# Softmax minus one-hot over 8192 rows: moving the middle blocks' loads and stores from two queues to one

## The chip, the cores and the metric

The kernel runs on one core of one Trainium2 chip. The metric is device time in microseconds (us); lower is better. The core has four compute engines that matter here: VectorE (DVE in the profile), ScalarE (ACT), GpSimd (POOL) and, for a tiny transpose at the start, TensorE (PE). SyncE (SP) only issues transfers. Data moves between the off-chip memory (HBM) and the on-chip memory (SBUF, 128 partitions) over 16 DMA engines. Two engines issue transfers in this kernel, SP and ACT, each into a queue of its own: the profile calls SP's queue q1 and ACT's q10. A transfer is issued by an instruction in its engine's stream, so an engine that waits before an issue holds up whatever stands behind it in that stream.

## What is computed

This is the backward pass of a cross-entropy loss. For each of 8 x 1024 rows of 8192 logits, the output is the row's softmax, less 1 at the place of the row's label.

```python
def reference(logits, labels):
    logits_max = np.max(logits, axis=-1, keepdims=True)
    exp_logits = np.exp(logits - logits_max)
    softmax = exp_logits / np.sum(exp_logits, axis=-1, keepdims=True)
    ...
    one_hot[batch_idx, seq_idx, labels] = 1.0
    return (softmax - one_hot).astype(np.float32)
```

Logits and output are float32, 268.4 MB each; every element is read once and written once.

## The kernel before, in words

The 8192 rows of the matrix are cut into 32 blocks of 256 rows (`B = 32`). Within a block, partition p holds the rows 2p and 2p+1, which lie one after the other in HBM. The kernel calls `t = 2b` and `u = 2b + 1` the two "rows" of block b: a row is thus a tile of 128 partitions x 8192 elements, 4 MB, one run of 32 KB for each partition. A whole block is 8 MB, one run of 64 KB for each partition.

The tile `X` (line 47) has three slots of one block each (`SLOTS = 3`). Block b uses slot b mod 3, and all the work is done in place: the logits are loaded into `X`, overwritten by exponentials, scaled, the one-hot subtracted, and the result is stored from the same place. So block b+3 can be loaded only once block b has been stored.

`by_block(b)` (line 258) writes out the work of a block in one fixed order:

- GpSimd and VectorE build the one-hot rows, GpSimd for the last 2048 columns (`hot_pool`), VectorE for the first 6144 (`hot`, in PSUM), as bytes packed four to a word.
- VectorE takes the row's maximum (`m`), which is where the row's load is waited for; ScalarE takes the exponential and its sum (`s`); VectorE takes the reciprocal (`r`).
- VectorE scales and subtracts in 6144 columns (`finish_dve`). The other 2048 are scaled by GpSimd for row t and by ScalarE for row u, and GpSimd subtracts (`subtract_pool`).
- `move(b)` issues the block's stores and a later block's loads. In the last block row t's store is issued as soon as it is finished, ahead of `move`.

All waits are written by hand through `run` (line 72), which puts an instruction on an engine with the semaphores that it waits for. `finished[t]` holds what a store of row t waits for (VectorE's and GpSimd's last results), `stored[t]` what a load into the same place waits for, `loaded[t]` what the maximum waits for. `got` and `put` are the semaphores of loads and stores.

Six row loads are issued on SP at the start (three blocks). Then, by `move` (line 154):

- Blocks 0 and 1: the two rows are stored on ACT, one transfer each. After block 0, block 3's two rows are loaded on SP, each when the row three blocks before it has been stored.
- Blocks 2 to 25 (`TURN <= b < RETURN`): the block is stored in two halves at once, the even partitions on SP and the odd ones on ACT (`halves`, line 124), each 64 runs of 64 KB. Behind each store, on the same queue, the half load of block b+2 is issued, which waits until its own half of block b-1 has been stored. After block 25, block 28's rows are also loaded on SP.
- Blocks 26 to 31: rows are stored on ACT, and on SP row t+6 is loaded when row t has been stored.

Which places of `move` set the order matters below:

```python
            if TURN <= b < RETURN:
                store(ts, halves)
                load([t + G * (SLOTS - 1) for t in ts], halves)
            else:
                for t in ts:
                    if t not in stored:
                        store([t], [(nc.scalar, every)])
            if b < TURN - 1 or b >= RETURN - 1:
                for t in ts:
                    if t + G * SLOTS < T:
                        load([t + G * SLOTS], [(nc.sync, every)])
```

Of the kernel before, what the change touches and what calls it, by code (L numbers as in the profile page):

```python
# [7 lines left out]
P = 128  # L8
G = 2
SLOTS = 3  # L10


TURN, RETURN = 2, 26
POOLED = 2048
ONE = 56.0
BYTE = mybir.dt.float8e4
# [3 lines left out]
def kernel(  # L20
# [6 lines left out]
    nc = tc.nc  # L27
# [9 lines left out]
    T = N // P  # L37
# [27 lines left out]
    with tc.tile_critical():  # L65
        sem = tc.alloc_semaphore
        got = [[sem(f"got{i}{j}") for j in range(G)] for i in range(SLOTS)]
        put = [[[sem(f"put{i}{j}{h}") for h in range(2)] for j in range(G)] for i in range(SLOTS)]
        lab_got, dve, act, pe, pool = (sem(n) for n in ("lab_got", "dve", "act", "pe", "pool"))
        count = {}  # L70

        def run(engine, waits, counter, method, **operands):

            last = {}
            for counted, value in waits:
                last[counted.name] = counted, max(value, last.get(counted.name, (counted, 0))[1])
            waits = list(last.values())
            for w in waits[:-1]:
                engine.wait_ge(*w)  # L79
            instruction = getattr(engine, method)(**operands)  # L80
            for w in waits[-1:]:
                instruction._wait_ge(*w)
            step = 16 if method == "dma_start" else 1
            instruction.then_inc(counter, step)
            count[counter.name] = count.get(counter.name, 0) + step
            return counter, count[counter.name]
# [3 lines left out]
        w = run(nc.gpsimd, [], pool, "memset", ap=ident[:], constant=0.0)  # L90
# [12 lines left out]
        for j in range(G):  # L103
            w = run(
                nc.tensor, [w_ident, w_lab], pe, "transpose",
                out=lab_ps[:, j, :], in_=lab_f[:, j, :], identity=ident[:],
            )
        w_turned = run(nc.vector, [w], dve, "tensor_copy", out=lab_i[:], in_=lab_ps)

        def small(w, out, in0, scalar1, scalar2, op0, op1):  # L110
            return run(
                nc.vector, [w], dve, "tensor_scalar",
                out=out[:], in0=in0[:], scalar1=scalar1, scalar2=scalar2, op0=op0, op1=op1,
            )

        w = small(w_turned, low, lab_i, 1, None, Alu.bitwise_and, Alu.bypass)
        w = small(w, place, low, 255.0 * ONE, ONE, Alu.mult, Alu.add)
        w = small(w, low, lab_i, 2, None, Alu.bitwise_and, Alu.bypass)
        w = small(w, lab, low, 32767.5, 1.0, Alu.mult, Alu.add)
        w = run(nc.vector, [w], dve, "tensor_tensor", out=place[:], in0=place[:], in1=lab[:], op=Alu.mult)  # L120
        w = small(w, low, lab_i, 2, None, Alu.logical_shift_right, Alu.bypass)
        w_lab = run(nc.vector, [w], dve, "tensor_copy", out=lab[:], in_=low[:])

        halves = [(nc.sync, slice(0, P, 2)), (nc.scalar, slice(1, P, 2))]
        loaded, stored, finished = {}, {}, []
        stored[-1] = [(0, w_turned), (1, w_turned)]

        def load(ts, queues):
            b, js = ts[0] // G, slice(ts[0] % G, ts[-1] % G + 1)
            for queue, ps in queues:  # L130
                free = [w for t in ts for h, w in stored.get(t - G * SLOTS, []) if ps.step is None or h in (None, ps.start)]
                w = run(
                    queue, free, got[b % SLOTS][js.start], "dma_start",
                    out=X[ps, b % SLOTS, js, :], in_=x_b[b, ps, js, :],
                )
            for t in ts:
                loaded[t] = w

        def store(ts, queues):
            b, js = ts[0] // G, slice(ts[0] % G, ts[-1] % G + 1)  # L140
            for t in ts:
                stored[t] = []
            for h, (queue, ps) in enumerate(queues):
                w = run(
                    queue, [w for t in ts for w in finished[t]],
                    put[b % SLOTS][js.start][h], "dma_start",
                    out=o_b[b, ps, js, :], in_=X[ps, b % SLOTS, js, :],
                )
                for t in ts:
                    stored[t].append((ps.start, w))  # L150

        every = slice(None)

        def move(b):
            ts = [G * b, G * b + 1]
            if TURN <= b < RETURN:
                store(ts, halves)
                load([t + G * (SLOTS - 1) for t in ts], halves)
            else:
                for t in ts:  # L160
                    if t not in stored:
                        store([t], [(nc.scalar, every)])
            if b < TURN - 1 or b >= RETURN - 1:
                for t in ts:
                    if t + G * SLOTS < T:
                        load([t + G * SLOTS], [(nc.sync, every)])

        def row(t):
            return X[:, t // G % SLOTS, t % G, :]
# [12 lines left out]
        def row_max(t):  # L182
            maxima[t] = maximum([loaded[t]], m[:, t : t + 1], row(t))

        def row_max_around(t, between):
            w_first = maximum([loaded[t]], m_half[:, 0:1], row(t)[:, : V // 2])
            made = between()
            w_second = maximum([loaded[t]], m_half[:, 1:2], row(t)[:, V // 2 :])
            maxima[t] = run(
                nc.vector, [w_first, w_second], dve, "tensor_tensor",  # L190
                out=m[:, t : t + 1], in0=m_half[:, 0:1], in1=m_half[:, 1:2], op=Alu.min,
            )
            return made
# [12 lines left out]
        def one_hot_pool(t):  # L206
            last_pool[:] = [one_hot(nc.gpsimd, pool, last_pool, t, hot_pool[:, t % G, :], slice(PART, V // 4))]

        def scale_pool(t, w):
            x = row(t)[:, pooled]  # L210
            return run(
                nc.gpsimd, [w], pool, "tensor_scalar",
                out=x, in0=x, scalar1=r[:, t : t + 1], scalar2=None, op0=Alu.mult,
            )
# [11 lines left out]
        def one_hot_dve(t):  # L226
            return one_hot(nc.vector, dve, used.get(t % G, [w_words, w_lab]), t, hot[:, t % G, :], slice(0, PART))
# [10 lines left out]
        def row_exp(t):  # L238
            x = row(t)
            return run(  # L240
                nc.scalar, [maxima[t]], act, "activation",
                out=x, in_=x, func=Act.Exp, bias=m[:, t : t + 1], scale=1.0, accum_out=s[:, t : t + 1],
            )

        def row_recip(t, w):
            return run(nc.vector, [w], dve, "reciprocal", out=r[:, t : t + 1], in_=s[:, t : t + 1])

        def scale_act(t, w, c):
            x = row(t)[:, c]
            return run(  # L250
                nc.scalar, [w], act, "activation",
                out=x, in_=x, func=Act.Copy, bias=0.0, scale=r[:, t : t + 1],
            )
# [4 lines left out]
        def by_block(b):  # L258
            t, u = G * b, G * b + 1
            one_hot_pool(t)  # L260
            one_hot_pool(u)
            t_hot = one_hot_dve(t)
            u_hot = one_hot_dve(u)
            row_max(t)
            w_exp = row_exp(t)
            if b + 1 < B:
                row_max(u)
                t_sum = row_recip(t, w_exp)
                w_exp = row_exp(u)
                w_scaled = scale_pool(t, t_sum)  # L270
            else:
                t_sum = row_max_around(u, lambda: row_recip(t, w_exp))
                w_scaled = scale_act(t, t_sum, pooled)
                w_exp = row_exp(u)
            t_pool = subtract_pool(t, w_scaled)
            finished.append([finish_dve(t, [t_hot, t_sum]), t_pool])
            if b + 1 == B:
                store([t], [(nc.scalar, every)])
            u_sum = row_recip(u, w_exp)
            u_pool = subtract_pool(u, scale_act(u, u_sum, pooled))  # L280
            finished.append([finish_dve(u, [u_hot, u_sum]), u_pool])
            move(b)

        for t in range(G * SLOTS):
            load([t], [(nc.sync, every)])
        for b in range(B):
            by_block(b)
        for b in range(B - SLOTS, B):
            for t in (G * b, G * b + 1):
                for _, w in stored[t]:  # L290
                    nc.scalar.wait_ge(*w)


# [28 lines left out]
```

## Time and profile before

| | |
|---|---|
| time, median of 3 runs | 1258.59 us (1258.44 to 1258.67) |
| the profiled execution's own time | 1258.22 us |
| its span, first to last instruction | 1256.4 us |
| VectorE busy | 1101.3 us (88%) |
| GpSimd busy | 549.1 us (44%) |
| ScalarE busy | 529.1 us (42%) |
| row maximum on VectorE | 64 rows, 8.68 us each |
| scale and subtract on VectorE | 64 rows, 6.62 us each |
| exponential on ScalarE | 64 rows, 7.12 us each |
| DMA packets | 12343, of them 2064 under 512 B |

Some help with the views of the profile. The page divides the span into 40 slices of 31.4 us and gives the busy share of each in tenths, and the GB/s that the DMA engines moved. The windows do the same for stretches that one asks for; there each row has the stretch, its length, the busy time and (in brackets) the number of instructions of TensorE's matmuls and weight loads, VectorE, ScalarE and GpSimd, then the clock granted to TensorE, the DMA engines' busy share and GB/s. A packet is counted in the stretch in which it starts, so in stretches of a few microseconds share and rate can be off, and a share can be a little over 1. A line such as "DVE m L80 <- DMA X<-in_logits_dram: 109.4, 27, 8.9" reads: VectorE's instructions that write `m` waited for loads of `X` for 109.4 us in all, 27 times, 8.9 us at the longest. All compute instructions have line 80, where `run` issues them.

The transfers as issued (the last number is the median time from issue to landing):

```profile
X<-in_logits_dram SPq DMA_DIRECT2D x16, 4096.0 KB, 37.2
out_dram<-X ACTq DMA_DIRECT2D x16, 4096.0 KB, 35.5
out_dram<-X ACTq DMA_DIRECT2D x24, 27.0
out_dram<-X SPq DMA_DIRECT2D x24, 24.1
X<-in_logits_dram SPq DMA_DIRECT2D x24, 40.7
X<-in_logits_dram ACTq DMA_DIRECT2D x24, 46.1
```

The first two lines are rows, the other four the halves of blocks.

### The profile page before, as it was taken

To read this page: it belongs to the slowest core of one execution; us is meant where nothing else is said; L and a number is where in the kernel's file an instruction comes from. 1 tells how busy PE (TensorE), PEld (TensorE's weight loads), DVE (VectorE), ACT (ScalarE), POOL (GpSimd) and SP (SyncE) were. 2 spreads that over 40 slices of the span, in tenths; PEclk is the share of its full clock that TensorE was granted. 3 is DMA by queue.
4 is the path that set the end of the run, shared out by engine and by line. 5 is a ranking of instruction groups with operands and counts; after the bars stand their busy time and mean duration, and the time that the engine had idled before them with its cause. 6 is when DMAs were issued, how large, how long until landed. Compare 5 with 4: busy or idle time off the path is not lost.

```text
span 1256.4 us, 893 instructions
## 1 busy us (share of the span) xinstructions
PE 0.4 (0%) x2; PEld 0.3 (0%) x2; DVE 1101.3 (88%) x267; ACT 529.1 (42%) x162; POOL 549.1 (44%) x166
## 2 busy tenths in 40 slices
PE   0000000000000000000000000000000000000000
PEld 0000000000000000000000000000000000000000
DVE  7999878889888898888988889888898888999984
ACT  2444542345523455234553345533455333555432
POOL 2555522555335553355533455334553345544331
DMA  9999999999999999999999999999999999999998
GB/s 403 417 434 451 432 434 432 434 432 434 426 413 432 434 434 434 432 434 413 424 434 434 434 432 432 407 432 434 432 428 411 432 434 416 433 434 434 428 433 364
DMA packets 12343, 537.00 MB, mean 427 GB/s; under 512 B 2064, under 2 KB 2064, under 8 KB 2096
## 3 DMA queue, kind: packets, MB, share of 16 engines
q10 hardware_dynamic: 6192, 268.51, 50.1%
q1 hardware_dynamic: 6144, 268.44, 49.6%
q14 instruction: 7, 0.06, 0.0%
HBM read 268.50 MB, written 268.44 MB: 427 GB/s over the span
## 4 chain that ended last, share of the span: by engine, by line
DMA 54%; DVE 32%; ACT 9%; another core or an unknown queue 2%; POOL 1%; ACTq 0%; issue 0%; SPq 0%
DMA X<-in_logits_dram 48%; DVE m L80 21%; ACT X L80 9%; DVE X L80 8%; DMA out_dram<-X 6%; DVE hot L80 1%; POOL X L80 1%; DVE m_half L80 1%; ACTq L80 0%; DVE r L80 0%; SPq L80 0%; ACTq L79 0%; SPq L317 0%; SPq L65 0%
## 5 line engine op out<-in xcount | busy, mean ns | idle before, releaser
L80 ACT ACTIVATE X<-X,m 128x8192 f32<-128x8192 f32 x64 | 455.8, 7122 | 697.0 <-DVE m L80 697.0
L80 DVE TENSOR_REDUCE m<-X 128x1 f32<-128x8192 f32 x63 | 544.5, 8680 | 109.4 <-DMA X<-in_logits_dram 109.4
L80 POOL TENSOR_SCALAR X<-X,r 128x2048 f32<-128x2048 f32 x31 | 168.7, 5441 | 643.6 <-DVE r L80 643.6
L80 DVE SCALAR_TENSOR_TENSOR X<-X,r,hot 128x6144 f32<-128x6144 f32 x64 | 423.3, 6615 | 2.2
L80 POOL TENSOR_TENSOR X<-X,hot_pool 128x2048 f32<-128x2048 f32 x64 | 245.3, 3833 | 35.4 <-ACT X L80 28.4
L80 POOL TENSOR_SCALAR hot_pool<-words,lab,place 128x512 int32<-128x512 int16 x64 | 132.9, 2076 | 10.9 <-DVE lab L80 4.5
L80 DVE TENSOR_SCALAR hot<-words,lab,place 128x1536 int32<-128x1536 int16 x64 | 117.0, 1874 | 0.0
L80 ACT ACTIVATE X<-X,r 128x2048 f32<-128x2048 f32 x33 | 66.1, 2002 | 8.4 <-DVE r L80 8.4
L80 DVE RECIPROCAL r<-s 128x1 f32<-128x1 f32 x64 | 10.1, 159 | 18.2 <-ACT X L80 18.2
L80 DVE TENSOR_REDUCE m_half<-X 128x1 f32<-128x4096 f32 x2 | 8.8, 4410 | 3.8 <-DMA X<-in_logits_dram 3.8
L80 ACT ACTIVATION_READ_ACCUMULATOR X<-X,m 128x1 f32 x64 | 11.9, 186 | 0.0
L80 DVE CAST X<-lab_raw 32x256 f32<-32x256 int32 x1 | 0.4, 373 | 4.8 <-DMA lab_raw<-in_labels_dram 4.8
L80 ACT ACT_TABLE_LOAD x1 | 1.3, 1283 | 1.3 <-SPq L65 1.3
L80 POOL IOTA words<- 128x2048 int16 x1 | 1.8, 1823 | 0.0
L80 DVE TENSOR_TENSOR m<-m_half 128x1 f32<-128x1 f32 x1 | 1.6, 1598 | 0.0
L80 DVE TENSOR_SCALAR low<-lab_i 128x64 int32<-128x64 int32 x3 | 0.6, 195 | 0.1
L80 DVE CAST lab_i<-hot 128x64 int32<-128x64 f32 x1 | 0.2, 224 | 0.5 <-PE hot L80 0.5
L80 PE MATMUL hot<-ident,X 32*128 32x32 f32 x2 | 0.4, 299 | 5.2 <-DVE X L80 5.2
L80 POOL MEMSET ident<- 32x32 f32 x1 | 0.1, 115 | 0.5 <-SPq L65 0.5
L80 PEld LDWEIGHTS hot<-ident,X 32*128 32x128 f32 x2 | 0.3, 194 | 5.2 <-DVE X L80 5.2
L80 DVE TENSOR_TENSOR place<-place,lab 128x64 f32<-128x64 f32 x1 | 0.2, 224 | 0.0
L80 POOL TENSOR_SCALAR_AFFINE_SELECT ident<-ident 32x32 f32<-32x32 f32 x1 | 0.2, 202 | 0.1
(7 smaller groups left out, 1.0 us busy)
## 6 DMA issues: line engine op xcount, KB each, us to landing
X<-in_logits_dram SPq DMA_DIRECT2D x16, 4096.0 KB, 37.2
out_dram<-X ACTq DMA_DIRECT2D x16, 4096.0 KB, 35.5
out_dram<-X ACTq DMA_DIRECT2D x24, 27.0
out_dram<-X SPq DMA_DIRECT2D x24, 24.1
X<-in_logits_dram SPq DMA_DIRECT2D x24, 40.7
X<-in_logits_dram ACTq DMA_DIRECT2D x24, 46.1
lab_raw<-in_labels_dram ACTq DMA_DIRECT2D x1, 64.0 KB, 3.9
```

What stands on the lines that cost most here:

```text
L80: instruction = getattr(engine, method)(**operands)
```

## The change

The halves go. From block 3 on, every transfer is issued by SP, in one order. ACT issues only the row stores of blocks 0, 1 and 2.

- Blocks 0 to 2 (`TURN` is 3 now) are stored by row on ACT. After blocks 0 and 1, blocks 3 and 4 are loaded by row on SP.
- Blocks 3 to 25: one transfer stores the whole block, the next loads the whole of block b+2, both on SP, 128 runs of 64 KB each. The load waits for block b-1 to have been stored. After block 25, row 56 (block 28) is loaded too.
- Blocks 26 to 31: for each row t in turn, SP stores it and then loads row t+5, which waits for the store of row t-1. Rows 59 to 63 are followed by no load.

On SP the instructions are thus: 10 row loads; 23 times a block's store and a block's load; a row load; 7 times a row's store and a row's load; 5 row stores. The stores' semaphores are one for each place instead of two. The compute instructions of all engines stay as they are and in their order.

```diff
-TURN, RETURN = 2, 26
+TURN, RETURN = 3, 26
...
-        put = [[[sem(f"put{i}{j}{h}") for h in range(2)] for j in range(G)] for i in range(SLOTS)]
+        put = [[sem(f"put{i}{j}") for j in range(G)] for i in range(SLOTS)]
...
-                free = [w for t in ts for h, w in stored.get(t - G * SLOTS, []) if ps.step is None or h in (None, ps.start)]
+                free = [w for t in ts for w in stored.get(t - G * SLOTS, [])]
...
         every = slice(None)
+        on_sp, on_act = [(nc.sync, every)], [(nc.scalar, every)]
 
         def move(b):
             ts = [G * b, G * b + 1]
             if TURN <= b < RETURN:
-                store(ts, halves)
-                load([t + G * (SLOTS - 1) for t in ts], halves)
-            else:
+                store(ts, on_sp)
+                load([t + G * (SLOTS - 1) for t in ts], on_sp)
+                if b == RETURN - 1:
+                    load([G * (b + SLOTS)], on_sp)
+                return
+            for t in ts:
+                if b < TURN:
+                    store([t], on_act)
+                elif t not in stored:
+                    store([t], on_sp)
+                if b >= RETURN and t + G * SLOTS - 1 < T:
+                    load([t + G * SLOTS - 1], on_sp)
+            if b < TURN - 1:
                 for t in ts:
-                    if t not in stored:
-                        store([t], [(nc.scalar, every)])
-            if b < TURN - 1 or b >= RETURN - 1:
-                for t in ts:
-                    if t + G * SLOTS < T:
-                        load([t + G * SLOTS], [(nc.sync, every)])
+                    load([t + G * SLOTS], on_sp)
...
             if b + 1 == B:
-                store([t], [(nc.scalar, every)])
+                store([t], on_sp)
```

More of the change, by code (lines that the diff above doesn't have):

```diff
@@ L122 @@
         w_lab = run(nc.vector, [w], dve, "tensor_copy", out=lab[:], in_=low[:])
-        halves = [(nc.sync, slice(0, P, 2)), (nc.scalar, slice(1, P, 2))]
         loaded, stored, finished = {}, {}, []
-        stored[-1] = [(0, w_turned), (1, w_turned)]
+        stored[-1] = [w_turned]
         def load(ts, queues):
@@ L142, in store @@
                 stored[t] = []
-            for h, (queue, ps) in enumerate(queues):
+            for queue, ps in queues:
                 w = run(
                     queue, [w for t in ts for w in finished[t]],
-                    put[b % SLOTS][js.start][h], "dma_start",
+                    put[b % SLOTS][js.start], "dma_start",
                     out=o_b[b, ps, js, :], in_=X[ps, b % SLOTS, js, :],
@@ L149, in store @@
                 for t in ts:
-                    stored[t].append((ps.start, w))
+                    stored[t].append(w)
         every = slice(None)
+        on_sp, on_act = [(nc.sync, every)], [(nc.scalar, every)]
         def move(b):
@@ L284 @@
         for t in range(G * SLOTS):
-            load([t], [(nc.sync, every)])
+            load([t], on_sp)
         for b in range(B):
@@ L289 @@
             for t in (G * b, G * b + 1):
-                for _, w in stored[t]:
+                for w in stored[t]:
                     nc.scalar.wait_ge(*w)
```

## The prediction

> **What bounds the kernel now.** I read the page's rows on the transfers first, then the waits, the chain, windows by stage, and the transfers of two single stretches.
>
> ```profile
> DMA  9999999999999999999999999999999999999998
> ...
> q10 hardware_dynamic: 6192, 268.51, 50.1%
> q1 hardware_dynamic: 6144, 268.44, 49.6%
> HBM read 268.50 MB, written 268.44 MB: 427 GB/s over the span
> ```
>
> The 16 DMA engines are busy in every slice, and the two queues (q1 is SP's, q10 is ACT's) together fill 99.7% of them. The bytes don't change, so the time is bytes by rate plus whatever the engines lose. VectorE, the busiest engine at 88%, is not the bound: it waits for loads.
>
> ```profile
> DVE m L80 <- DMA X<-in_logits_dram: 109.4, 27, 8.9
> ```
>
> So the question is where the rate is below its best. The windows (after the five engines' busy times come the clock, the DMA share and GB/s):
>
> ```profile
> 36.00:48.00 12.00, 0.00 (x0) 0.00 (x0) 11.40 (x5) 4.90 (x3) 11.57 (x5) 1.00 1.00 393
> 78.00:117.00 39.00, 0.00 (x0) 0.00 (x0) 38.37 (x10) 16.43 (x5) 21.31 (x7) 1.00 1.00 433
> 117.00:312.00 195.00, 0.00 (x0) 0.00 (x0) 170.11 (x41) 82.16 (x25) 84.93 (x26) 1.00 1.01 435
> 312.00:1014.70 702.70, 0.00 (x0) 0.00 (x0) 616.17 (x144) 295.76 (x90) 309.25 (x90) 1.00 1.00 428
> 1066.00:1215.00 149.00, 0.00 (x0) 0.00 (x0) 142.06 (x33) 68.50 (x21) 69.04 (x20) 1.00 1.01 434
> 1226.00:1238.00 12.00, 0.00 (x0) 0.00 (x0) 11.21 (x4) 9.22 (x3) 2.42 (x2) 1.00 0.88 380
> ```
>
> Row-by-row traffic, loads on SP and stores on ACT at once (78 to 117 and 1066 to 1215), runs at 433 to 434 GB/s. The long middle stage, in halves, runs at 428 though the engines count as busy: packets are stretched there. Only the stretch near the end (1226 to 1238) has idle engines, at a share of 0.88: rows 60 and 61 are out and row 62's store is issued only at 1233.03. The price per block of the middle stage comes from the chain, where VectorE's first maximum of a block starts when that block's load lands (start, duration):
>
> ```profile
> 358.49 17.29 DVE m L80 x2
> ...
> 1062.42 17.29 DVE m L80 x2
> ```
>
> Eighteen blocks lie between: (1062.42 - 358.49) / 18 = 39.11 us each. A block moves 2 x 256 rows x 32 KB = 16.78 MB, which at 434 GB/s is 38.66 us. So each block loses 0.45 us. In it both queues carry stores, then both carry loads, so it has one turn from loads to stores and one back; that is all that sets it apart from the row stages, so I charge the 0.45 to that pair of turns.
>
> **The change, part by part.** *Bytes and packets.* Nothing is added; runs of 64 KB stay runs of 64 KB. Block 4 now loads by row, as blocks 0 to 3 do: no cost, since row traffic shows the better rate.
>
> *One queue in place of two.* Can one feed 16 engines? Between 5 and 40 us only SP's queue has work:
>
> ```profile
> DMA packets 512, 15.20 MB, mean 434 GB/s; under 512 B 48, under 2 KB 48, under 8 KB 48
> ...
> q1 hardware_dynamic: 512, 15.20, 100.9%
> ```
>
> Yes, with several transfers' ends inside that stretch, so the end of one transfer costs the next nothing. The trace of before has no pure one-queue turn from store to load. From below its price x is 0: the row stages alternate loads and stores and lose nothing (434). From above, take a transfer that starts with nothing ahead of it: the first row load takes 12.3 us to land and a 4.19 MB row at 434 GB/s takes 9.7, so 2.6 us, as if the engines ran dry at every turn. The nearest row is the middle stage, 0.45, since there both queues turn almost together. Almost: the median store half lands after 24.1 us on SP and 27.0 on ACT, the load half after 40.7 and 46.1 (section 6), and a 64 KB packet takes 65,536 x 16 / 434e9 s = 2.4 us. So one queue still runs one or two packets the old way when the other has turned, and between 117 and 312 us, with the same stage, the rate was a full 435. With one queue this cover is gone. I take x = 0.5, a little above the nearest row.
>
> *How many turns.* After: blocks 3 to 25 give 23 pairs (store b, load b+2); rows 52 to 58 give 7 more (store t, load t+5); rows 59 to 63 are stores alone. 30 pairs x 0.5 = 15.0 us added. Removed: the middle stage's losses, 19 blocks (7 to 25) x 0.45 = 8.6; blocks 2 to 6 showed no loss.
>
> *The seam at block 26.* Where ACT's row stores first meet loads, the rate dips: 36 to 48 us at 393, which is 12 x (434 - 393) / 434 = 1.1 us. That one stays. The same meeting comes again where before goes back to rows (about 1054 us), which I price alike at 1.1; after has none there. Removed: 1.1.
>
> *The end.* The idle stretch before store 62 costs 12 x (434 - 380) / 434 = 1.5 us. After, from the end T of block 26's load, SP's order puts store 25, load 27, then row transfers of 9.7 us each: row 63's load ends at T+184, and stores 59, 60 and 61 keep the engines busy to T+213. VectorE runs blocks 28 to 31 back to back at 34.8 us (as before does between 1093.71 and 1163.40) and frees row 62 at about T+208 and row 63 at T+215, ahead of their turns at T+213 and T+223. No gap: 1.5 removed.
>
> *Waits on SP's queue.* SP now waits for each block's last result, then for stored(b-1), with nothing else behind it. In the middle stage it has room: the store of a block is issued at 428.95 while the next load lands at 436.55, 7.6 us later; less the 2.6 of a cold start, 5.0 us of work still lie in the queue when the new store joins. Load b+2 waits for a store that finished before load b+1 began moving, so it is issued with the store. In the row stage load t+5 waits for store t-1 with load t+4 and store t, 19.4 us, still ahead of it. Hidden, then; if that cover were gone, up to 2.6 us each, 30 times. ScalarE loses some 1.4 us of issuing a block (0.51 and 0.84); it is idle 58% of the span, so nothing.
>
> *Sum.* 15.0 - 8.6 - 1.1 - 1.5 = +3.8 us on the profiled span of 1256.4, so 1260.2. The median of the runs, 1258.59, lies 2.2 above that span: 1262.4.
>
> The split middle stage ran at 428 and the one-queue stretch at 434. The Trainium skill ("DMA: Bandwidth & Descriptors", section "Rules for kernel authors") says two transfers to disjoint partition halves use the same engines and should be one transfer. That would put joined and split at one price; by it the sum is 30 x 0.45 - 11.2 = +2.3, 1260.9. The same page ("Two DMAs through the same engine are not ordered") says that descriptors of one queue start in order but are pipelined; that speaks against the dry-run price, and the 434 GB/s of SP's queue alone agrees for loads after loads, while no row here shows a load after a store.
>
> **The rivals.** *Turns are free in one queue* (x from 0 to 0.29): for it, the row stages and the one-queue stretch at 434; against it, those never turn all engines at once. At x = 0: -11.2, so 1245.2 and 1247.4. This is the other side; it decides from x below 0.29, where 30x falls 2.5 us short of 11.2. *The turn costs what it costs now* (x 0.29 to 0.45): within 0.2%, at 0.37 just 1258.5. *Turns are dear* (x about 1): 30 - 11.2 = +18.8, 1277.4; for it, the cover of the second queue is lost; against, the stretch is only 0.45 with most engines in step. *The engines run dry at each turn* (2.6): +66.8, 1325; against it, the 5.0 us of queued work. That the change doesn't do what it says I exclude: the order of instructions shows 23 whole-block pairs on SP.
>
> **How the numbers follow.** Forecast (x 0.45 to 0.8): 0.36. Free turns 0.31; the same price 0.19; dear 0.11; dry 0.03. A difference under 0.2%, 2.5 us, cannot be told from none. Faster 0.31, same 0.19, slower 0.50 (the forecast and the two dear cases). The forecast alone spans 1261 to 1271. Range: 1246 (free turns, and a little below for the start) to 1281 (x = 1.1).
>
> **What would show it.** Right: one window per block with a rate of some 427 in the middle, VectorE's maxima starting 39.1 to 39.3 us apart, the row stage of the end below 434 (it turns 7 times), no idle stretch near 1226 to 1238. Wrong: 434 in the middle and 38.7 us apart (turns are free), a DMA share below 1 in each block (the queue ran dry), or loads that land later than VectorE's 35 us of work allows in the row stage.

## The result, and the profile after

The changed kernel takes 1256.73 us (median of 14 runs, 1255.40 to 1257.75) against 1258.63 us for the kernel before (14 runs, 1258.05 to 1260.42): a ratio of 0.9982, 95% interval 0.9973 to 0.9990. It is a little faster, 1.9 us; the prediction said 1262.4 and slower. The profiled execution has a span of 1254.9 us against 1256.4.

The page of the changed kernel, transfers first:

```profile
DMA  9999999999999999999999999999999999999997
...
q1 hardware_dynamic: 10944, 511.71, 94.9%
q10 hardware_dynamic: 912, 25.23, 4.7%
```

SP's queue now carries 95% of the bytes, and the engines still count as busy all the time: one queue feeds them. VectorE waits for loads about as before:

```profile
DVE m L80 <- DMA X<-in_logits_dram: 101.7, 24, 10.0
```

The windows of the changed kernel in the stretches shown of before (DMA share and GB/s are last):

```profile
78.00:117.00 39.00, 0.00 (x0) 0.00 (x0) 38.37 (x10) 16.43 (x5) 21.31 (x7) 1.00 1.00 430
117.00:312.00 195.00, 0.00 (x0) 0.00 (x0) 172.31 (x42) 82.16 (x25) 87.13 (x27) 1.00 1.01 435
312.00:1014.70 702.70, 0.00 (x0) 0.00 (x0) 618.01 (x145) 295.75 (x90) 311.02 (x91) 1.00 1.00 430
1058.00:1068.00 10.00, 0.00 (x0) 0.00 (x0) 9.08 (x2) 0.36 (x1) 0.00 (x0) 1.00 1.00 393
1066.00:1215.00 149.00, 0.00 (x0) 0.00 (x0) 143.51 (x36) 73.47 (x23) 69.04 (x20) 1.00 1.01 434
1226.00:1238.00 12.00, 0.00 (x0) 0.00 (x0) 7.68 (x3) 3.63 (x3) 3.83 (x1) 1.00 1.01 434
```

Three things are to be seen. The middle stage went from 428 to 430, where a fall to about 427 was expected. The row stage at the end runs at 434, although it now turns seven times between loads and stores on one queue: its rate is the row stage's of before (434), so those turns add nothing. And the seam, a stretch at 393 that opens the row stage, is still there (1058 to 1068).

The chain gives the price of a block again. VectorE's first maxima after a load, in the changed kernel:

```profile
278.56 17.29 DVE m L80 x2
...
1058.92 17.29 DVE m L80 x2
```

(1058.92 - 278.56) / 20 = 39.02 us a block; the kernel before has 280.43 and 1062.42 for the same two blocks (7 and 27), 39.10. Against 38.66 at 434 GB/s that is a loss of 0.36 us a block instead of 0.44.

The last line of the windows concerns the idle stretch that before showed between 1226 and 1238, and that the change closed (380 to 434 GB/s). The kernel before issued its last two stores here (start, duration of the issue):

```profile
1233.03 0.34 ACTq L80 DMA_DIRECT2D out_dram<-X  x1
...
1240.60 0.34 ACTq L80 DMA_DIRECT2D out_dram<-X  x1
```

For each of the two the trace gives the time from issue to landing:

```profile
DMA to landing us min/median/max: 12.4/12.4/12.4
...
DMA to landing us min/median/max: 14.5/14.5/14.5
```

They landed at 1245.4 and 1255.1. The two stores ahead of them were issued at 1195.51 and 1200.12 and took 30.6 and 35.7 us: landed at 1226.1 and 1235.8. So the kernel's last four stores land 9.7 us apart, which is what a row takes at 434 GB/s, straight across the stretch in which the packet records show idle engines. The packets of the trace say why: the 16 engines are not in step. At 1232.0 nine of them have a packet under way, and at 1233.0 two, with the store that lands at 1235.8. A transfer has landed when its last engine is done; its last data packet ends 0.3 us earlier, at 1254.81 for the last store of before and at 1253.34 for that of the changed kernel. So the share of 0.88 is a mean over engines of which the early ones waited and the late ones, which set the time, did not. In the changed kernel the last four land at 1224.7, 1234.3, 1244.1 and 1253.7, the same 9.7 apart. Nothing was there to be won.

How far the engines are out of step can be read in the trace from the 16 increments that it records as each transfer lands. For the last store the first and the last of them lie 1.5 us apart in the kernel before and 6.0 in the changed one, whose engines stop one after another from 1247.7 on. The early engines' wait for store 62 in the kernel before brought them closer again: 3.6 us for the store ahead of it, 1.5 for it. In GB/s, a mean over all engines, none of this is seen.

### The profile page after: what moved, and what is told of

Its sections match the earlier page's. It is cut to its first block, busy times and chain, and to the rows that moved or that the text cites. A ratio compares the mean times of both kernels' runs of the same rounds, so it can differ in the third digit from the quotient of the medians.

```text
span 1254.9 us, 821 instructions
## 1 busy us (share of the span) xinstructions
PE 0.4 (0%) x2; PEld 0.3 (0%) x2; DVE 1101.0 (88%) x267; ACT 529.1 (42%) x162; POOL 549.1 (44%) x166
## 4 chain that ended last, share of the span: by engine, by line
DMA 49%; DVE 37%; ACT 12%; SPq 0%; issue 0%; ACTq 0%
DMA X<-in_logits_dram 45%; DVE m L80 25%; ACT X L80 12%; DVE X L80 10%; DMA out_dram<-X 4%; DVE hot L80 2%; DVE m_half L80 0%; SPq L80 0%; DVE r L80 0%; SPq L79 0%; SPq L322 0%; ACTq L79 0%; SPq L65 0%
```

## The experiments

Each run was compared with runs of the kernel before on the same chip. Ratios are to that kernel.

**Which part pays: the middle or the end?** First the end alone. The middle keeps its halves; the last six blocks go on SP as in the changed kernel.

```diff
                 load([t + G * (SLOTS - 1) for t in ts], halves)
...
+                if b == RETURN - 1:
+                    load([G * (b + SLOTS)], [(nc.sync, every)])
+                return
+            for t in ts:
+                if t not in stored:
+                    store([t], [(nc.scalar if b < TURN else nc.sync, every)])
+                if b >= RETURN and t + G * SLOTS - 1 < T:
+                    load([t + G * SLOTS - 1], [(nc.sync, every)])
...
```

> The kernel before with only the last six blocks changed: their row stores and row loads go on SP in the changed kernel's order, the middle keeps the halves on two queues. If the idle stretch before the last but one store was worth 1.5 us, and the row stage's turns cost nothing in one queue, 1257.1 (1.5 below before). If the gain came from the middle stage alone, 1258.6, as before. If one queue's turns cost 0.5 us there, 1260.6.

Measured: 1260.43 us, ratio 1.0009 (1.0000 to 1.0018). No gain from the end. The median is that of the third expectation, but its reason isn't seen: between 1100 and 1210 us this run moves 433 GB/s, as the row stage of before does (432). Then the middle alone: the changed kernel with the last six blocks as before.

```diff
-                    load([G * (b + SLOTS)], on_sp)
+                    for t in ts:
+                        load([t + G * SLOTS], on_sp)
...
-                    store([t], on_sp)
-                if b >= RETURN and t + G * SLOTS - 1 < T:
-                    load([t + G * SLOTS - 1], on_sp)
+                    store([t], on_act)
+            if b >= RETURN:
+                for t in ts:
+                    if t + G * SLOTS < T:
+                        load([t + G * SLOTS], on_sp)
...
```

> The changed kernel with the last six blocks as before (row stores on ACT, loads of row t+6 on SP); blocks 3 to 25 in whole blocks on SP. If the idle stretch that the packet records show before the last but one store costs nothing, because stores land back to back across it (9.67, 9.68 and 9.67 us apart in the kernel before), the median is that of the changed kernel, 1256 to 1258. If closing that stretch was worth 1.5 us, 1258 to 1259.

Measured: 1261.23 us, ratio 1.0016 (1.0004 to 1.0028), which neither expectation had. The two mixtures are no faster than either pure kernel, the second clearly slower than both. The windows of this run show that the two parts don't add up:

```profile
200.00:1010.00 810.00, 0.00 (x0) 0.00 (x0) 716.98 (x167) 345.04 (x105) 359.62 (x104) 1.00 1.00 433
1100.00:1210.00 110.00, 0.00 (x0) 0.00 (x0) 105.57 (x25) 49.30 (x15) 51.83 (x15) 1.00 1.00 424
1226.00:1238.00 12.00, 0.00 (x0) 0.00 (x0) 11.17 (x5) 8.88 (x3) 2.84 (x1) 1.00 0.41 177
```

and those of the kernel before:

```profile
200.00:1010.00 810.00, 0.00 (x0) 0.00 (x0) 711.04 (x166) 343.67 (x105) 353.00 (x102) 1.00 1.00 429
1100.00:1210.00 110.00, 0.00 (x0) 0.00 (x0) 106.49 (x25) 49.30 (x15) 51.78 (x15) 1.00 1.00 432
```

The middle on one queue ran at 433 here, better than in the changed kernel's own profile; the end, the same code as before, ran at 424 instead of 432 while the engines count as busy. Here, too, the engines fall out of step, by up to 12.9 us between the first and the last increment of a transfer (6.2 in the kernel before, 7.1 in the changed one). That is the share of 0.41 in the last window: its four last stores still land 9.7 us apart, at 1228.1, 1237.8, 1247.5 and 1257.1. So the same code moved its packets at different rates in different surroundings; what decides it is not shown. Single parts therefore can't be priced by swapping them, and the idle-gap question rests on the landings above, not on these two runs.

**What makes a turn dear: the length of a run?** In the changed kernel the rows of X are padded, so that whole-block transfers have runs of 32 KB, as row transfers have.

```diff
-    X = const.tile([P, SLOTS, G, V], fp32)
+    X_wide = const.tile([P, SLOTS, G, V + 16], fp32)
+    X = X_wide[:, :, :, :V]
```

> The changed kernel with X padded by 64 bytes a row, so that whole-block transfers consist of runs of 32 KB instead of 64 KB; order, number and size of the transfers stay. Theory A (the loss at a turn between loads and stores belongs to the 64 KB runs): the middle stage's period between blocks falls from 39.02 us towards 38.7 us, some 7 us less in all, median about 1249. Theory B (it belongs to the length of a stretch in one direction, 19 us for a block against 9.7 for a row): period stays at 39.0, median 1256 to 1258. Theory C (a cost of every turn that the row stage only hides elsewhere): as B.

Measured: 1258.69 us, ratio 0.9996 (0.9987 to 1.0005), and 430 GB/s in the middle as in the changed kernel:

```profile
312.00:1014.70 702.70, 0.00 (x0) 0.00 (x0) 615.68 (x144) 295.77 (x90) 308.98 (x90) 1.00 1.00 430
```

Theory A falls.

**Or the length of a stretch in one direction?** The changed kernel's row-by-row order of the last blocks, from block 3 on, all on SP:

```diff
-TURN, RETURN = 3, 26
+TURN, RETURN = 3, 3
...
+            elif b == TURN - 1:
+                load([G * (b + SLOTS)], on_sp)
```

> The changed kernel with the row-by-row order of its last six blocks used from block 3 on, all on SP: store row t, load row t+5, 32 KB runs, a turn every 9.7 us, twice as many turns. Theory A (64 KB runs) and theory B (length of a stretch in one direction) both expect the rate of the row stage, 433 GB/s, throughout: some 8 to 9 us less, median 1247 to 1249. Theory C (every turn costs the 0.36 us that a pair costs in the middle stage): 58 turns instead of 30, about 10 us more than the changed kernel, 1266.

Measured: 1252.12 us, ratio 0.9947 (0.9935 to 0.9960), with 433 GB/s in the middle although the turns are twice as many:

```profile
312.00:1014.70 702.70, 0.00 (x0) 0.00 (x0) 621.57 (x145) 295.76 (x90) 310.89 (x90) 1.00 1.00 433
```

Theory C, a fixed price for every turn, falls: it wanted 1266. The opposite test: stretches of 9.7 us, but with 64 KB runs, by halves of 64 partitions in turn, both on SP.

```diff
-                store(ts, halves)
-                load([t + G * (SLOTS - 1) for t in ts], halves)
+                for half in halves:
+                    store(ts, [half])
+                    load([t + G * (SLOTS - 1) for t in ts], [half])
```

> Blocks 3 to 25 in halves of 64 partitions on SP alone, in turn: store even half, load even half, store odd half, load odd half; 64 KB runs, stretches in one direction of 9.7 us; start and last six blocks as in the changed kernel. Theory B (length of the stretch): turns nearly free, period 38.7 to 38.8, median 1249 to 1253. Theory A2 (64 KB runs make a turn dear however long the stretch): twice as many turns, period 39.4, 1264. Theory D (transfer size): as B.

Measured: 1267.71 us, ratio 1.0061 (1.0038 to 1.0084), 425 GB/s in the middle:

```profile
312.00:1014.70 702.70, 0.00 (x0) 0.00 (x0) 609.16 (x142) 293.76 (x89) 302.47 (x88) 1.00 1.00 425
```

That is 16.78 MB / 425 = 39.48 us a block, 0.82 lost over two pairs of turns, 0.41 a pair. A stretch of half the length makes a turn no cheaper, so for these transfers theory B falls too. The dear turns cost about 0.4 a pair with 8 MB and with 4 MB transfers; the cheap ones are those of row transfers.

**Rows in pairs.** The order and the stretches of the changed kernel, each whole-block transfer replaced by its two row transfers:

```diff
-                store(ts, on_sp)
-                load([t + G * (SLOTS - 1) for t in ts], on_sp)
+                for t in ts:
+                    store([t], on_sp)
+                for t in ts:
+                    load([t + G * (SLOTS - 1)], on_sp)
```

> The changed kernel with each whole-block transfer of blocks 3 to 25 replaced by its two row transfers in the same order: store t, store u, load, load, all on SP, 32 KB runs. The stretches in one direction stay 19 us long, the transfers are 4 MB like those of the row-by-row order. Theory B (a turn is dear after a long stretch in one direction): the losses at the turns stay, period 39.0 us, median 1257 to 1260. Theory D (the loss belongs to 8 MB transfers, or to how few transfers are queued): the rate of the row-by-row order, period 38.75, median 1251 to 1253.

Measured: 1254.65 us, ratio 0.9962 (0.9950 to 0.9973), between the two expectations, and 432 GB/s:

```profile
312.00:1014.70 702.70, 0.00 (x0) 0.00 (x0) 620.83 (x145) 295.77 (x90) 310.63 (x90) 1.00 1.00 432
```

The chain is less kind than the window: VectorE's first maxima of blocks 8 and 26 start at 307.44 and 1008.64, 38.96 us a block, 0.30 lost. With rows in turn (1252.12 us, above) blocks 7 and 27 start at 258.58 and 1033.00, 38.72, 0.06 lost over two pairs of turns. So among row transfers the length of a stretch isn't out of it.

Two transfers of 4 MB again, but by halves of the partitions in place of rows (store, store, load, load; 32 KB runs by padding). The lines are against the run by halves in turn:

```diff
                 for half in halves:
                     store(ts, [half])
+                for half in halves:
                     load([t + G * (SLOTS - 1) for t in ts], [half])
```

> Blocks 3 to 25 on SP as store even half, store odd half, load even half, load odd half, 32 KB runs by padding: two 4 MB transfers for each stretch of 19 us, like the run with row pairs (1254.7), but each transfer walks partition by partition through both rows. If two 4 MB transfers in place of one of 8 MB are what made the turns cheap there: 1253 to 1256. If walking row by row over all partitions is: 1257 to 1260, as with whole blocks of 32 KB runs (1258.7).

Measured: 1258.79 us, ratio 0.9994 (0.9985 to 1.0004), 430 GB/s:

```profile
312.00:1014.70 702.70, 0.00 (x0) 0.00 (x0) 615.65 (x144) 295.76 (x90) 308.95 (x90) 1.00 1.00 430
```

The two runs have the same run length, transfer size, queue and stretches. They differ in the walk, as the code names it: a row transfer goes through the partitions with one run each, the other takes both runs of a partition before the next. By their ratios the first takes 4.0 us less. They also differ in the partitions of a transfer (128 against 64) and in the padding; but the padded whole blocks, with 128 partitions, took the same 1258.7, and the next run has 32 KB runs without padding. Whether HBM addresses are behind that was tried by giving partition p the rows p and 128+p in the changed kernel (`"(b j p) v -> b p j v"` for both tensors, and the labels to match):

> The changed kernel with another assignment of rows: partition p of a block holds rows p and 128+p instead of 2p and 2p+1, so a whole-block transfer has two runs of 32 KB per partition, 4 MB apart in HBM, in place of one of 64 KB; the transfers, their order and the work stay. Theory E (what a turn costs depends on which HBM addresses the ending and the starting stream use at the same moment): the loss per pair of turns in blocks 3 to 25 moves away from 0.36 us, up or down, by more than 0.1; median below 1254 or above 1260. Theory F (a turn of a whole block costs 0.36 us whatever the addresses): period 39.0, median 1256 to 1259 (32 KB runs cost up to 2 us more by their 1213 ns a packet).

Measured: 1259.47 us, ratio 1.0005 (0.9997 to 1.0014), 429 GB/s in the middle: no cheaper with the two runs 4 MB apart than side by side (1258.69). Theory E falls for turns on one queue.

**Both directions at once.** All loads on SP, all stores on ACT, so that there are no turns. By halves of even and odd partitions with 64 KB runs:

```diff
-                store(ts, halves)
-                load([t + G * (SLOTS - 1) for t in ts], halves)
+                store(ts, [(nc.scalar, ps) for ps in halves])
+                load([t + G * SLOTS for t in ts], [(nc.sync, ps) for ps in halves])
...
```

> All loads on SP, all stores on ACT, so that both directions run at once throughout; blocks 0 to 25 in halves of 64 partitions with 64 KB runs (loads from block 3 on), each half load waiting for the store of its own half three blocks before; last six blocks by row as in the kernel before. Theory B: no stretch in one direction, so no loss, 38.65 us a block, and 64 KB runs move a row in 2418 instead of 2 x 1213 ns a packet, some 3 us less than rows on two queues (1248.2): 1245 to 1247. Theory A2 (64 KB runs are what makes turns dear): no better than rows on two queues, 1250 or more. A rival: slots come free too late and the engines idle: above 1252.

Measured: 1426.69 us, ratio 1.1237 (1.1200 to 1.1274), far above every time that was expected. Its executions differ widely (1407.7 to 1517.9) and the profiled one was the longest, so its lines show the kind of loss, not the size:

```profile
312.00:1014.70 702.70, 0.00 (x0) 0.00 (x0) 487.19 (x115) 230.03 (x70) 248.57 (x73) 1.00 0.90 344
```

Engines that are busy 0.90 of the time should move 390 GB/s; they moved 344, so packets were stretched: a 64 KB packet took 2.75 us on average there and 2.44 in the changed kernel. The queues ran dry as well; that slots came free too late would explain it and is not shown. Two edits mend it. With rows p and 128+p on a partition (32 KB runs at other addresses):

> The run by direction in halves, with rows p and 128+p on partition p (32 KB runs, 4 MB apart). Theory E: the stretching changes much, rate while busy above 400, under 1330. Theory F2 (both directions at once over the same halves of the partitions is what stretches): 1400 as before it.

Measured: 1248.37 us, ratio 0.9914 (0.9901 to 0.9927). And with the old addresses and 32 KB runs by padding:

> The run by direction in halves of even and odd partitions (1427) with X padded by 64 bytes a row: runs of 32 KB, the rows, addresses, order and transfers as there. The run with rows p and 128+p (1248) changed the run length and the addresses at once. If the length of a run was it: 1248 to 1252. If the addresses were it: 1400 and more as before.

Measured: 1248.65 us, ratio 0.9914 (0.9899 to 0.9929), 433 GB/s throughout:

```profile
312.00:1014.70 702.70, 0.00 (x0) 0.00 (x0) 622.56 (x146) 296.06 (x91) 310.91 (x90) 1.00 1.00 433
```

So here the length of the run decides, not the addresses. Whole blocks of 128 partitions with 64 KB runs, by direction:

> Loads on SP and stores on ACT as in the run by direction, but whole blocks of 128 partitions instead of halves of 64, 64 KB runs. If the stretched packets there came from the halves (64 of 128 partitions at a time in each direction), the rate while busy returns to 433 and only waits for slots are left: 1250 to 1290. If both directions at once with 64 KB runs stretch the packets, it stays near 1400.

Measured: 1259.04 us, ratio 1.0020 (0.9997 to 1.0043), 430 GB/s: 64 KB runs are this bad by halves only, and even whole they are not as good as 32 KB runs by direction.

**Rows on two queues, throughout.** The kernel before with its own last-blocks scheme for all blocks: one constant (`TURN, RETURN = 26, 26`).

> The kernel before with its own row-by-row scheme used for all blocks: loads on SP, stores on ACT, 32 KB runs, load of row t+6 when row t is stored. Theories A and B: rate 433 throughout, 1247 to 1250 as long as loads come in time. A rival: with both queues sharing the engines evenly a store takes 19.4 us instead of 9.7, slots come free later, and VectorE waits for loads with the engines idle at times: above 1258.

Measured: 1248.18 us, ratio 0.9913 (0.9897 to 0.9928). Its windows have 433 GB/s from block 3 to the end:

```profile
312.00:1014.70 702.70, 0.00 (x0) 0.00 (x0) 621.88 (x145) 299.78 (x92) 310.86 (x90) 1.00 1.00 433
1066.00:1215.00 149.00, 0.00 (x0) 0.00 (x0) 131.91 (x33) 60.29 (x20) 64.89 (x20) 1.00 1.00 433
```

With rows p and 128+p it is the same:

> The row-by-row kernel on two queues (1248.2) with rows p and 128+p on partition p: a row transfer is then one contiguous stretch of 4 MB in HBM. Theory E allows any change, and 1248 if these streams don't meet; if the good rate comes from alternating directions row by row alone, 1248 as it was; if one contiguous 4 MB stretch a transfer makes streams meet, above 1252.

Measured: 1248.03 us, ratio 0.9921 (0.9903 to 0.9939). Rows on two queues beat both kernels, by some 8.5 us the changed one.

## Why the prediction was wrong

*What was right.* Transfers are the bound; one queue feeds all 16 engines; the queue never runs dry in the middle; the head, ScalarE's freed time and the waits on SP cost nothing. Most of the loss is in stretched packets at constant busy share, as read from the windows.

*The step that failed* is the price of a turn, in the paragraph "One queue in place of two": x = 0.5 for all 30 pairs, "a little above the nearest row", because the second queue's cover is lost. The changed kernel's whole-block pairs cost 0.36 over the 20 blocks timed (39.02 - 38.66), less than the 0.44 of the halves on two queues. (Rows on two queues take 38.76 a block, from 261.38 to 1036.60 for the same 20; against that the two prices are 0.26 and 0.34, and the difference stays.) Losing the second queue's cover was to raise the price, and the price fell. And the seven row pairs cost nothing: 434 GB/s. The signs named ahead fell between: 430 and 39.02 us, neither the 427 and 39.1 to 39.3 of the forecast nor the 434 and 38.7 of free turns. Blocks 3 to 6 show no loss either (435 between 117 and 312 us, as before). So 7.2 us (20 x 0.36) stand where 15.0 was charged. The mistake behind it was to price all turns alike. The row stages' 434 was set aside because they "never turn all engines at once"; the runs show that row transfers turn cheaply on one queue as well (1252.1 with twice the turns), while transfers that take both of a partition's runs in succession cost 0.36 to 0.45 a pair by the windows (430 and 429 GB/s), at either run length.

*The credits.* The seam at block 26 (1.1) was credited as gone; it stayed, at 393 GB/s. The idle stretch at the end (1.5) was credited; it was no loss, as the landings 9.7 us apart show: the engines that set the time had no gap there. The middle's removed loss was put at 8.6; at 0.44 for the 20 blocks timed it is 8.8.

*The sum with the measured terms:* 7.2 - 8.8 = -1.6 us, against -1.9 between the medians. The predicted +3.8 differs from it by 7.8 too much for turns, less 2.6 of credits that were not there, and 0.2 too little for the loss removed. The two errors had opposite signs, so the total missed by less than the turns did. The agreement of -1.6 with -1.9 is in size only: a window's edges could hide a part of a microsecond in blocks 2 to 6, and the same middle ran at 430 in one execution and 433 in another (the mixture above), so a tenth of a microsecond a block is about as far as one profile carries.

*The rivals.* "Turns are free" and "the turn costs what it costs now" both hold a part: 0.36 for the blocks timed and 0 for rows, an average of 0.24 over 30 pairs, which lies in the first one's range. The prices drawn from lost cover and from a dry queue had no part in it. Of the Trainium skill's rule weighed there ("DMA: Bandwidth & Descriptors", "Rules for kernel authors": two halves on disjoint partitions should be one transfer) the direction agrees, 0.36 against 0.44, though the number of queues changed with it; on one queue, halves and whole blocks with 32 KB runs took the same time (1258.8 and 1258.7).

*What stays open.* Why walking a partition's two runs in succession makes a turn dear, why 64 KB runs by halves stretch when both directions are under way, and why the same end ran at 424 once and 432 once. Rows on one queue (1252.1) and on two (1248.2) also differ by 4 us at the same rate in the windows. Most of that is engines out of step: the last store's increments lie 5.7 us apart on one queue and 1.8 on two, and the last of them comes 4.0 and 1.3 us after the mean of the 16. Why the engines drift apart, on one queue and in the halves of before, is open.

## What to carry to other kernels

Where transfers are the bound and the engines never idle, look for windows whose GB/s is below the kernel's own best at the same busy share, and copy the transfer pattern of the best window to the rest before designing a new one: here one constant did that, for 10 us. Price a cost from a row that has the same shape of transfer, not from the nearest in time. The DMA share and GB/s are means over 16 engines, and the slowest engine sets the time: before crediting an idle stretch in the share, check when the transfers land.

## What the runs showed of the hardware that was not expected

The 16 engines drift out of step: the increments of one transfer lay up to 7.1 us apart in the changed kernel, 1.9 with rows on two queues (1248.2 us), and 12.9 in one mixture. Four stores therefore landed 9.7 us apart across stretches with a busy share of 0.88 and of 0.41 over 12 us, because the late engines had packets under way throughout. Loads and stores at once, in halves of 64 partitions, moved 344 GB/s in the longest execution with 64 KB runs and 433 with 32 KB runs (medians 1426.7 and 1248.7 us), with the same bytes, order and HBM addresses. On one queue, in whole blocks, run length made no such difference (430 and 430 GB/s).
